# One list schedule for the whole attention part of a hybrid encoder block: every instruction recorded with a duration, ordered in the source, then issued

## The chip, the core and the metric

The kernel runs on one core of a Trainium2 chip. The core has five instruction queues that matter here: TensorE (PE, matrix products and transposes into PSUM), VectorE (DVE), ScalarE (ACT), GpSimd (POOL) and SyncE (SP, which here only issues transfers). Each queue runs its instructions in the order in which the program has them, and waits at an instruction until what it needs is there. The metric is the device time of one execution in microseconds (us); lower is better.

## The reference

One layer on x of 2048 rows by 1024 columns, float32:

```python
u = rms_norm(h, norm1_w)
proj = u @ w_in                     # 3072 columns: dq dk dv | sq sk sv
# differential attention, 4 heads: two softmax maps per head on QK-normed q, k,
# position bias by bucket, chunk-causal mask
p = softmax(logits); attn = p[0] - lam * p[1]; y_diff = rms_norm(attn @ dv) * (1 - lambda_init)
# stick-breaking attention, 8 heads, strictly causal, no softmax
log_1mb = where(mask, log_sigmoid(-z), 0)
rem = cumsum(log_1mb, reverse=True) - log_1mb
a = where(mask, exp(log_sigmoid(z) + rem), 0);  y_sb = rms_norm(a @ sv)
h = h + concat(y_diff, y_sb) @ w_out
h = h + (silu(rms_norm(h) @ w_gate) * (rms_norm(h) @ w_up)) @ w_down
```

## The kernel before

**Tiles.** Rows are cut into 16 tiles of 128 (`NT`). Every large product is made from float16 halves: an operand is split into a high half and a low half (what the high half leaves), and three products, high by high, high by low and low by high, are summed in PSUM. Splitting is therefore work of its own everywhere: a cast for the high half (ACT, at times DVE or POOL) and a subtract for the low half (DVE or POOL).

**Stages.** Attention runs over eight groups (`NG`). Groups 0 to 3 are one differential head each, groups 4 to 7 two stick-breaking heads each. For each group there are

- the group's 384 columns of W_in, loaded, scaled and split (tiles `wst`, `w16`);
- the projection: for each of 16 row tiles the halves of the normed x come back from a DRAM scratch (`xt<-xs`, on SP) and 24 matmuls make `pj` (PE); from it come `qT`, `kT`, `v` (transposed by DMA and split);
- scores: for each tile i of 128 queries and each piece of up to 1024 keys, matmuls `sc<-kT,qT` into PSUM (PE);
- the weights: in the differential groups bias, maximum, exponential with sums, reciprocal and the difference of the two maps (DVE line 695, ACT line 685); in the stick-breaking groups a sigmoid on ACT and a running product along the row on DVE (the scan of lines 1123 and following), right to left;
- the split of the weights into halves (`s<-z` or `s16`) and their transposition to `aT`, mostly by a DMA transpose on SP (`aT<-s`, `aT<-z`, line 590 and 1173), in groups 4 to 6 for narrow pieces by transposes on PE, a cast on ACT and a subtract on DVE (lines 1141, 1145, 1149);
- values: matmuls `yp<-v,aT` (PE line 646), some pieces later than the scores; then a norm per head, and the mix row to a DRAM scratch `ms`.

The projection of group g + 1 runs beside the attention of group g. Near the end of group 7's projection the output weights are loaded in four quarters (`load_wo`; `WT` names the projection tiles at which the first three begin); then the output projection `po<-wo,mt` (line 1433) adds x and stores h. The last four row tiles' output projection overlaps the feed-forward part, which splits its weights in steps (`wg`, `wu`, `wd`) and is bound to the projections `pm` and `pd`.

**What sets the order.** Three different things:

- groups 0 to 3, the start of group 4, all of group 7's attention, the output projection and the feed-forward part are written as plain code, and the framework's scheduler orders it, by program order, priorities (`PRI`) and its own estimate of times;
- from tile 8 of group 4's projection up to group 7's eighth projection tile, `planned(4, NG - 2)` lists the work as tasks, each with an engine, a duration in ns, what it depends on, rooms it takes and gives back (a room is a buffer of one name) and a key (its due time in units of a group). `Plan.order` simulates five engines and one DMA ring, always takes the task with the smallest key that is ready, and the tasks are issued in that order under a manual schedule. The engine of each task is fixed by hand there;
- in the plain code, where an operation may go to one of several engines (casts `to16`, subtracts `tt`), `pick` keeps a running load for each engine and takes the one that would be loaded least, with weights `KW`:

```python
def pick(**cost):
    e = min(cost, key=lambda k: load[k] + cost[k] * KW[k])
    load[e] += cost[e] * KW[e]
```

In group 7 a piece's weights are always turned by DMA: `split_t` casts on ACT, subtracts on POOL, and one DMA transpose on SP turns both halves, whatever the piece's width; the value matmuls of a piece stand behind the last score matmul in issue (`issue_after(front[-1])`).

Of the kernel before, what the change touches and what calls it, by code (L numbers as in the profile page):

```python
# [25 lines left out]
NFG = FF // 256  # L26
# [36 lines left out]
class Task:  # L63
    __slots__ = ("eng", "ns", "fn", "deps", "get", "put", "key", "dma", "left", "users", "at", "end")

    def __init__(self, eng, ns, fn, deps, get, put, key, dma):
        self.eng, self.ns, self.fn, self.deps, self.get, self.put, self.key, self.dma = eng, ns, fn, deps, get, put, key, dma


class Claim:  # L70
    def __init__(self, name, n=1):
        self.name, self.n = name, n


class Plan:


    def __init__(self, room):
        self.tasks, self.room = [], dict(room)

    def add(self, eng, ns, fn, deps=(), get=(), put=(), key=0.0, dma=None):
        t = Task(eng, ns, fn, [d for d in deps if d is not None], get, put, key, dma)
        self.tasks.append(t)
        return t

    def order(self):
        for n, t in enumerate(self.tasks):
            t.users, t.at = [], None
            t.left = len(t.deps)
            t.key = (t.key, n)  # L90
        for t in self.tasks:
            for d in t.deps:
                d.users.append(t)
        events = [(0.0, n, "ready", t) for n, t in enumerate(self.tasks) if not t.left]
        heapq.heapify(events)
        count = len(self.tasks)
        ready = {e: [] for e in "TADPS"}
        free = {e: True for e in ready}
        after = {t: 0.0 for t in self.tasks}
        ring, done = 0.0, []  # L100
        while events:
            now = events[0][0]
            while events and events[0][0] <= now:
                _, _, kind, t = heapq.heappop(events)
                if kind == "ready":
                    ready[t.eng].append(t)
                elif kind == "idle":
                    free[t] = True
                else:
                    for c in t.put:  # L110
                        c.n -= 1
                        if not c.n:
                            self.room[c.name] += 1
                    for u in t.users:
                        u.left -= 1
                        after[u] = max(after[u], now + (0 if u.eng == t.eng else LAT[t.eng]))
                        if not u.left:
                            count += 1
                            heapq.heappush(events, (after[u], count, "ready", u))
            for e in ready:  # L120
                if not free[e]:
                    continue
                for t in sorted(ready[e], key=lambda t: t.key):
                    need = {}
                    for n in t.get:
                        need[n] = need.get(n, 0) + 1
                    if all(self.room[n] >= k for n, k in need.items()):
                        break
                else:
                    continue  # L130
                for n, k in need.items():
                    self.room[n] -= k
                ready[e].remove(t)
                t.at = now
                done.append(t)
                free[e] = False
                end = now + t.ns
                if t.dma is not None:
                    ring = max(ring, now) + t.dma
                    end = max(ring, now + t.ns + DMA_LAG)  # L140
                t.end = end
                count += 2
                heapq.heappush(events, (now + t.ns, count - 1, "idle", e))
                heapq.heappush(events, (end, count, "end", t))
        assert len(done) == len(self.tasks), (len(done), len(self.tasks), self.room, [t.key for e in ready for t in ready[e]][:20])
        return done


def block(tc, a, out):
    nc = tc.nc  # L150
    PE, ACT, DVE, POOL, SP = nc.tensor, nc.scalar, nc.vector, nc.gpsimd, nc.sync
    top = ExitStack()
    with top:
        cp = top.enter_context(tc.tile_pool(name="cp", bufs=1))
        sm = top.enter_context(tc.tile_pool(name="sm", bufs=8))
# [18 lines left out]
        def to16(dst, src, n, engines="ADP", psum=False):  # L174
            cost = {"A": 0.84 * n + 110, "D": (1.05 if psum else 0.53) * n + 70, "P": 1.1 * n + 80}
            e = pick(**{k: cost[k] for k in engines})
# [7 lines left out]
        def tt(dst, a_, b_, op, n, engines="DP"):  # L184
            cost = {"D": 1.15 * n + 70, "P": 2.45 * n + 80}
            e = pick(**{k: cost[k] for k in engines})
            (DVE if e == "D" else POOL).tensor_tensor(dst, a_, b_, op)  # L187

        def pri(k):
            def deco(f):  # L190
                @functools.wraps(f)
                def g(*args):
                    with tc.high_priority(PRI[k]) if PRI[k] else nullcontext():
                        return f(*args)
# [12 lines left out]
        make_identity(nc, id32[:])  # L207
        mhalf = c1(16, "mh")
# [1745 lines left out]
```

## Time and profile before

| | before |
|---|---|
| median of 3 runs | 2679.03 us (2674.0 to 2679.57) |
| profiled execution | 2680.29 us |
| its span in the trace | 2678.5 us, 50436 instructions |
| granted PE clock, mean | 0.977 of full speed |
| busy: PE, DVE, ACT, POOL | 93%, 69%, 46%, 50% |

Times are of one profiled execution. The span is the time between the first and the last instruction in the trace; the execution's own time is 1.8 us longer. PE's busy share counts its matmuls and transposes; its weight loads (PEld) run beside them. A wait row names who waited, for what, and on which tile, with the total in us, the number of times and the longest. A window row gives, for a stretch of the span, each engine's busy time in it. "SPq" is SP as a queue of transfers, the only thing that it does.

### The profile page before, as it was taken

What the parts mean: (1) busy time and instruction counts of PE and PEld (TensorE: products, weight loads), DVE (VectorE), ACT (ScalarE), POOL (GpSimd) and SP (SyncE); (2) the same over time, 40 slices, a digit from 0 to 9 for tenths busy, and PEclk for the clock granted to TensorE, in tenths of its full rate; (3) what the DMA queues carried; (4) which work ended last, traced back from release to release, by engine and by line L of the source; (5) the groups of instructions that cost most, each with busy time, mean ns of one, the idle gap of its engine ahead of it and who ended that gap; (6) DMA issues with size and microseconds to landing.
All of it is one profiled execution on the core that took longest, in us unless ns stands there. A gap on an engine that the chain in (4) does not pass through costs nothing.

```text
span 2678.5 us, 50436 instructions
## 1 busy us (share of the span) xinstructions
PE 2489.6 (93%) x19876; PEld 1517.9 (57%) x19876; DVE 1851.8 (69%) x3400; ACT 1243.0 (46%) x2378; POOL 1340.4 (50%) x1024
## 2 busy tenths in 40 slices
PE   6998989887999989689989899999999999999999
PEld 4655656566787876468775344444444444444444
DVE  6888879896788888676656868777685444444434
ACT  4655656555677867464534535344352112111121
POOL 2568677763453545455554656565564232322323
PEclk8999999999999999899999899999999999999999
DMA  6777697766797979998897574665649744635532
GB/s 222 214 153 178 150 199 167 166 137 157 159 184 177 183 155 190 199 198 224 217 292 271 208 255 179 250 229 200 246 183 346 292 179 143 232 143 185 195 111 94
DMA packets 574653, 526.52 MB, mean 197 GB/s; under 512 B 431104, under 2 KB 503296, under 8 KB 564176
## 3 DMA queue, kind: packets, MB, share of 16 engines
q1 hardware_dynamic: 572592, 521.22, 69.0%
q8 instruction: 155, 2.54, 0.4%
q0 software_dynamic: 512, 1.36, 0.2%
q10 hardware_dynamic: 1312, 0.72, 0.1%
q14 instruction: 82, 0.67, 0.1%
HBM read 261.08 MB, written 147.32 MB: 152 GB/s over the span
## 4 chain that ended last, share of the span: by engine, by line
PE 40%; DVE 7%; issue 2%; DMA 1%; ACT 1%; POOL 1%; SPq 0%; DVEq 0%; ACTq 0%; POOLq 0%
PE pd L1746 15%; PE pm L1638 10%; PE pd L1638 7%; PE pa L1638 7%; PE po L1433 1%; DVE wd L298 1%; DVE wu L298 1%; DVE cg L1711 1%; PE fsc L1571 1%; DVE cg L187 0%; DVE wg L298 0%; DMA aT<-s 0%; DVE b L187 0%; DVE act L187 0%; ACT wu L293 0%
## 5 line engine op out<-in xcount | busy, mean ns | idle before, releaser
L1746 PE MATMUL pd<-wd,act 128*128 128x512 f16 x1764 | 390.5, 379 | 1.5 <-DVE cg L1679 1.4
L636 PE MATMUL sc<-kT,qT 128*128 128x512 f16 (+3 forms) x1280 | 326.3, 355 | 20.2 <-DVE z L671 5.1
L415 PE MATMUL pj<-w,xt 128*128 128x384 f16 x1728 | 324.3, 335 | 12.4 <-ACT xt L1284 5.2
L646 PE MATMUL yp<-v,aT 128*128 128x64 f16 (+1 forms) x4872 | 254.6, 205 | 64.6 <-DMA aT<-s 45.3
L1638 PEld LDWEIGHTS <-wg 128*128 128x128 f16 x1848 | 182.1, 99 | 225.6 <-issue 13.2
L1638 PEld LDWEIGHTS <-wu 128*128 128x128 f16 x1848 | 181.0, 98 | 220.0 <-issue 5.3
L646 PEld LDWEIGHTS <-aT 128*128 128x128 f16 x4896 | 228.6, 100 | 128.3 <-DMA aT<-s 59.6
L1746 PEld LDWEIGHTS <-act 128*128 128x128 f16 x1764 | 172.8, 98 | 209.2 <-issue 2.5
L187 POOL TENSOR_TENSOR s<-z,s 128x1024 f16<-128x1024 f32 (+7 forms) x144 | 241.4, 1686 | 84.2 <-ACT s L178 72.5
L187 POOL TENSOR_TENSOR act<-cg,act 128x512 f16<-128x512 f32 x112 | 148.5, 1336 | 263.6 <-ACT act L1705 151.5
L415 PEld LDWEIGHTS <-xt 128*128 128x128 f16 x1728 | 170.7, 100 | 132.0 <-issue 22.2
L187 POOL TENSOR_TENSOR hs<-hs,cu 128x512 f32<-128x512 f32 x99 | 130.9, 1330 | 170.3 <-DVE hs L1752 70.6
L1705 ACT CAST act<-cg 128x512 f16<-128x512 f32 x126 | 77.6, 618 | 239.4 <-DVE cg L1711 164.3
L1638 PE MATMUL pm<-X,wu 128*128 128x512 f16 x792 | 181.9, 382 | 3.3 <-DVE cg L1675 2.0
L1638 PE MATMUL pm<-X,wg 128*128 128x512 f16 x792 | 181.7, 382 | 0.0
L1164 POOL TENSOR_TENSOR z<-z,z 128x512 f16<-128x512 f32 (+3 forms) x96 | 102.4, 1069 | 152.8 <-ACT z L1160 140.5
L1752 DVE SCALAR_TENSOR_TENSOR hs<-pd,c,hs 128x512 f32<-128x512 f32 x136 | 98.8, 747 | 109.8 <-PE pd L1746 88.3
L671 DVE TENSOR_SCALAR_CACHE_REDUCE z<-sc,c 128x512 f32<-128x512 f32 (+3 forms) x256 | 161.1, 648 | 15.7 <-PE sc L636 14.9
L685 ACT ACTIVATE z<-z,ng 128x1024 f32<-128x1024 f32 (+4 forms) x192 | 170.7, 891 | 2.2
L1433 PEld LDWEIGHTS <-mt 128*128 128x128 f16 x1536 | 151.3, 100 | 34.4 <-issue 13.7
L636 PEld LDWEIGHTS <-qT 128*128 128x128 f16 x1280 | 110.9, 100 | 69.2 <-issue 19.7
L1433 PE MATMUL po<-wo,mt 128*128 128x256 f16 x1152 | 139.0, 277 | 7.4 <-DVE wo L1436 4.0
(344 smaller groups left out, 4994.0 us busy)
## 6 DMA issues: line engine op xcount, KB each, us to landing
xt<-xs SPq DMA_DIRECT2D x112, 512.0 KB, 4.4
hs<-hd SPq DMA_DIRECT2D x68, 512.0 KB, 4.6
hd<-hs SPq DMA_DIRECT2D x56, 512.0 KB, 4.8
split<-wg SPq DMA_DIRECT2D x11, 1792.0 KB, 7.8
split<-wu SPq DMA_DIRECT2D x11, 1792.0 KB, 6.7
split<-wd SPq DMA_DIRECT2D x11, 1792.0 KB, 6.9
wg<-split SPq DMA_DIRECT2D x11, 1792.0 KB, 7.2
wd<-split SPq DMA_DIRECT2D x11, 1792.0 KB, 11.5
```

What stands on the lines that cost most here:

```text
L187: (DVE if e == "D" else POOL).tensor_tensor(dst, a_, b_, op)
L415: last = PE.matmul(pj[:, :384], lhsT=xv[:, xi, kt, :], rhs=G["w"][:, wi, kt, :], start=n == 0, stop=n == 23)
L636: last = PE.matmul(sc[:, : 128 * w].rearrange("p (t n) -> p t n", n=P), lhsT=G["q"][i // 4][:, a_, i % 4, :], rhs=G["k"][q][:, b_, 0:w, :] ...
L646: PE.matmul(yp[:, y0 : y0 + wd], lhsT=aT[:, a_, :], rhs=v[:, v_ : v_ + wd], start=start and j == 0 and q == 0, stop=stop and j == nb - 1 a ...
L671: DVE.tensor_scalar(z[:, lo : lo + f], sc[:, :f], kz_d[:], None, op0=ALU.mult, op1=ALU.max, accum_out=mx[:, m, nx : nx + 1])
L685: ACT.activation(z[:, :n], z[:, :n], AF.Exp, bias=ng[:, m : m + 1], accum_out=(s2[:, m, b : b + 1] if nb > 1 else su[:, m : m + 1]))
L1164: POOL.tensor_tensor(u["s16"][:, nd + lo : nd + hi], src[:, so + lo : so + hi], u["s16"][:, lo:hi], ALU.subtract)
L1433: PE.matmul(po[:, sl], lhsT=mt[:, kt, P * xi : P * xi + P], rhs=wos[2 * h + n][wi][:, kt, :], start=q == 0, stop=q == 23)
L1638: front[0] = PE.matmul(ps_[:].rearrange("p (t n) -> p t n", n=P), lhsT=wv[:, wo, wi, 128 * kt : 128 * kt + 128], rhs=X[xo][:, :, xi, kt, : ...
L1705: ACT.copy(act[:, o, 0], src)
L1746: front[0] = PE.matmul(po[:], lhsT=act[:, ao, xi, 128 * j : 128 * j + 128], rhs=W["d"][:, wo, wi, :], start=start and u == 0 and q == 0, s ...
L1752: DVE.scalar_tensor_tensor(dst, po[:], kd[:], src, op0=ALU.mult, op1=ALU.add)
```

## The change

All of the attention part, from the start of the kernel to the output projection, is now first taken down and then issued. `Recorder` stands between the code and the engines: while it is on, each engine call makes an `Op` with a duration from `price`, a table by engine, operation, width, source (PSUM or SBUF) and table function; its dependencies are found by who last wrote and who still reads each element of each tile (`Bank`, `View`). PE's matmuls into one PSUM tile are tied into pieces of up to 680 ns. `order` is one simulation of five engines for the whole list, and `issue` calls the real engines in its order under a manual schedule:

```diff
+PIECE, LOOK = 680.0, 60
-PRI = {"sc": 0, "spl": 0, "pv": 0, "fin": 0, "pm": -200, "po": 0, "pb": 0, "lw": 0, "fr": 0, "at": 200, "ox": 0, "wm": 0}
+PRI = {"sc": 400, "spl": 400, "pv": 0, "fin": 0, "pm": -200, "po": 400, "pb": 400, "lw": 0, "fr": 400, "at": 200, "ox": 0, "wm": 0}
-WT = (8, 9, 10)
+WT = (4, 7, 10)
-KW = {"A": 1.0, "D": 1.0, "P": 1.0}
+KW = {"A": 1.0, "D": 2.5, "P": 0.6}
...
+    def price(self, eng, name, args, kw):
...
+            if name == "dma_start_transpose":
+                return 1000 + 0.375 * width(src), 222.0 * width(src) / P, None, False
...
+            if name == "tensor_tensor_scan":
+                return 110 + 2.29 * n, None, None, False
...
+            return 180 + 1.07 * n, None, None, not psum and name != "tensor_reduce"
...
+            for e in ready:
+                if till[e] > now:
+                    continue
...
+                for o in ready[e][:LOOK]:
+                    if not can(o):
+                        continue
...
+                    if o.alts:
+                        w = way(o, e, now)
...
+                    if w[4] if w else o.port:
+                        if shared > now:
+                            if e == "D" and want is None:
+                                want = o.key
+                            continue
...
+                if o.table is not None and o.table != table:
+                    table = o.table
+                    ns += 1300
+                end = till[e] = now + ns
...
+                if o.dma is not None:
+                    ring = max(ring, now) + o.dma
+                    end = max(ring, now + ns + DMA_LAG)
```

An engine that is free takes, among the first 60 ready operations by key (program order less the priority's boost), the first whose tiles have a free buffer (`can`). The model knows one DMA ring with 2300 ns from issue to landing, 1300 ns for a change of ACT's function table, and a port: an operation of DVE on SBUF alone and one of POOL on SBUF are not run at the same time (`port`, `shared`). Where an operation may go to several engines (`either`), the engine is chosen when it is ready, by who would end first, with the durations weighted by `KW` (`way`): an operation's time counts 2.5 times on DVE and 0.6 times on POOL.

`planned`, `Plan` and `Task` are gone; groups 4 to 7 all come from the plain code of `sb_attn`. There narrow pieces are turned on PE in all four groups, and `issue_after` is gone:

```diff
+            def turn_on(m, n):
+                return n <= 512 or (n < 1024 and m == 1)
...
-                        front.append(score_chunk(G, sc, i, 2 * b + c, m, w // P))
+                        score_chunk(G, sc, i, 2 * b + c, m, w // P)
...
-                    return n, split_t(om[:, :n], n, "A", "P", wide[0] if g < NG - 1 else None, g)
...
+                        if tee and c == 0:
+                            for k in range(nb):
+                                PE.transpose(sc[:, P * k : P * k + P], om[:, P * k : P * k + P], id32[:])
...
+                            ACT.copy(h_, sc[:, :w])
+                            DVE.tensor_tensor(l_, sc[:, :w], h_, ALU.subtract)
+                            continue
...
-                    with tc.issue_after(front[-1]):
-                        stage_c(i, m, b, n, aT)
...
-                        planned(4, NG - 2)
...
+            rec.issue()
```

In group 7 these are 64 transposes on PE, 22 casts on ACT and 22 subtracts on DVE, for 16 DMA transposes less. ACT has five table loads for three before. The feed-forward part is still ordered by the framework, and its `pick` uses the new `KW`; 14 of its subtracts `act<-cg,act` go from DVE to POOL.

Three places show what moves. In the rows a name is a tile and its number, then what is read, then partitions and elements; the new instructions of the attention part all have the line of `issue`, 514.

DVE, where the differential groups hand over to the stick-breaking groups. `z<-z,rc,z` is the difference of two softmax maps, `z<-sc,diag` the first scan of group 4, `qT`, `yk` and `v` are low halves of projections. Before:

```order
L695 SCALAR_TENSOR_TENSOR z_8151<-z_8170,rc_8198,z_8151 128x1024
L695 SCALAR_TENSOR_TENSOR z_8160<-z_8179,rc_8198,z_8160 128x1024
L484 SCALAR_TENSOR_TENSOR qT_7980<-pj_8257,qT_7980 64x256
L484 SCALAR_TENSOR_TENSOR v_7979<-sd_8331,v_7979 128x4x64
L484 SCALAR_TENSOR_TENSOR yk_8139<-pj_8257,kT_7981 64x256
L484 SCALAR_TENSOR_TENSOR vr_7324<-pj_8258,vr_7324 128x4x64
L484 SCALAR_TENSOR_TENSOR qT_7980<-pj_8257,qT_7980 64x256
L484 SCALAR_TENSOR_TENSOR yk_8139<-pj_8257,kT_7981 64x256
L898 SCALAR_TENSOR_TENSOR v_7979<-sd_8546,v_7979 128x4x64
L1123 SCALAR_TENSOR_TENSOR z_8555<-sc_8556,diag 128x128
```

And now:

```order
L514 SCALAR_TENSOR_TENSOR z_7989<-z_8179,rc_8410,z_7989 128x1024
L514 SCALAR_TENSOR_TENSOR z_8075<-z_8220,rc_8410,z_8075 128x896
L514 TENSOR_SCALAR z_8483,mx_8283<-sc_8351,c_189 128x512
L514 TENSOR_SCALAR z_8483,mx_8283<-sc_8384,c_189 128x256
L514 ISA z_8483,mx_8283<-sc_8384,bias,c_189 128x256
L514 ISA mx_8283 128x1
L514 TENSOR_REDUCE ng_8536<-mx_8283 128x2
L514 SCALAR_TENSOR_TENSOR yrs_8539<-yss_7479,er_7616 128x4
L514 SCALAR_TENSOR_TENSOR qT_8534<-pj_8314,qT_8534 64x256
L514 SCALAR_TENSOR_TENSOR z_8558<-sc_8412,diag 128x128
```

Before, the first scan stands behind the last difference of maps and a row of projection halves; now it stands in the middle of the last differential pieces, and two more differences of maps follow 26 rows behind it.

SP, in group 7 where the output weights come in (`z<-in_w_out_dram`). `xt<-xs` are the operands of the next projection tiles. Before:

```order
L1173 DMA_TRANSPOSE aT_17525<-z_17434 128x16x128
L1173 DMA_TRANSPOSE aT_17529<-s_17496 128x16x128
L590 DMA_TRANSPOSE aT_17663<-s_17660 128x2x128
L590 DMA_TRANSPOSE aT_17678<-s_17675 128x2x128
L590 DMA_TRANSPOSE aT_17689<-s_17686 128x4x128
L590 DMA_TRANSPOSE aT_17700<-s_17697 128x4x128
L1048 DMA qT_17450<-qT_17450 64x1024 x2
L1404 DMA z_17746<-in_w_out_dram 128x4x256
L1404 DMA z_17747<-in_w_out_dram 128x4x256
L1404 DMA z_17844<-in_w_out_dram 128x4x256
L1404 DMA z_17845<-in_w_out_dram 128x4x256
L237 DMA bias<-in_norm_w_dram 128x1024
```

And now:

```order
L514 DMA xt_17615<-xs 128x2048
L514 DMA_TRANSPOSE aT_17623<-s_17532 128x16x128
L514 DMA z_17727<-in_w_out_dram 128x4x256
L514 DMA z_17731<-in_w_out_dram 128x4x256
L514 DMA xt_17798<-xs 128x2048
L514 DMA xt_18001<-xs 128x2048
L514 DMA_TRANSPOSE aT_18017<-s_17848 128x10x128
L514 DMA_TRANSPOSE aT_18023<-s_17876 128x2x128
L514 DMA_TRANSPOSE qT_18040<-st_17493 128x8x128
L514 DMA_TRANSPOSE kT_18059<-st_17493 128x8x128
L514 DMA bias<-in_norm_w_dram 128x1024
L514 DMA ms<-mo_18047 128x2x256
```

The narrow transposes (2 and 4 blocks) at the head of group 7 are gone from the queue, and the quarters of the output weights stand apart, with projection operands between them.

POOL, at the end of the attention part. `x<-z,x` are low halves of the feed-forward part's operands, `sx`, `sq` and `wg<-stages` the first gate weight. Before:

```order
L187 TENSOR_TENSOR x_20989<-z_20976,x_20989 128x2x512
L233 TENSOR_TENSOR xrs_21248<-xrs_21248,mh_68 128x1
L187 TENSOR_TENSOR x_21390<-z_21244,x_21390 128x2x512
L187 TENSOR_TENSOR sx_21467<-stages 128x512
L233 TENSOR_TENSOR xrs_21373<-xrs_21373,mh_68 128x1
L187 TENSOR_TENSOR z_21389<-z_21245 128x512
```

And now:

```order
L514 TENSOR_TENSOR z_21259<-z_21476,z_21259 128x512
L220 TENSOR_SCALAR wg_21534<-stages,c_21531 128x2x512
L220 TENSOR_SCALAR wg_21534<-sx_21551,c_21531 128x512
L514 TENSOR_TENSOR x_21480<-z_21455,x_21480 128x2x512
L514 TENSOR_TENSOR x_21482<-z_21476,x_21482 128x2x512
L220 TENSOR_TENSOR sq_21532<-stages,sq_21532 128x512
```

POOL now has two wide subtracts of operands next to each other there, and the first gate weight's work stands between the operands' rows.

More of the change, by code (lines that the diff above doesn't have):

```diff
@@ L129, in order @@
                 else:
                     continue
[L131 to L141, printed above, removed]
+                for b in o.first:
+                    queue[b.slot].remove(b)
+                    room[b.slot] -= 1
@@ L207, in block @@
         make_identity(nc, id32[:])
+        rec.start()
         mhalf = c1(16, "mh")
```

890 lines of the change are left out of this document (415 added, 475 removed).

## The prediction

> **What bounds the kernel now.** I read the page's head and its busy shares first, then the table of busy time by stage, then TensorE's (PE's) own waits in each stage, and last the rows of the operations that the change moves.
>
> ```profile
> span 2678.5 us, 50436 instructions
> PE 2489.6 (93%) x19876; PEld 1517.9 (57%) x19876; DVE 1851.8 (69%) x3400; ACT 1243.0 (46%) x2378; POOL 1340.4 (50%) x1024
> ```
>
> PE is the busiest engine by far, but 93% is a mean over two unlike halves, so the table by stage decides. Its columns are the stage's length, then busy time (and instructions) of PE, PE's weight loads, DVE, ACT and POOL, then the granted clock, the DMA share and GB/s. I cut where the kind of work changes: start, four differential groups, the change to the stick-breaking groups, groups 4 to 6, group 7 as the output weights come in, the output projection, the first feed-forward step, and the rest.
>
> ```profile
> 0.00:67.00 67.00, 45.31 (x233) 28.14 (x234) 43.78 (x117) 31.08 (x60) 17.90 (x32) 0.90 0.70 222
> 67.00:603.00 536.00, 485.83 (x4074) 321.27 (x4072) 463.41 (x1331) 318.22 (x828) 375.15 (x269) 0.98 0.76 171
> 603.00:670.00 67.00, 51.39 (x747) 46.29 (x745) 44.33 (x96) 35.68 (x83) 25.20 (x19) 0.92 0.64 159
> 670.00:1072.00 402.00, 369.69 (x5876) 308.08 (x5875) 342.24 (x479) 291.65 (x603) 195.04 (x181) 0.98 0.88 175
> 1072.00:1206.00 134.00, 104.43 (x1092) 72.15 (x1090) 89.42 (x144) 72.17 (x146) 63.62 (x50) 0.87 0.92 197
> 1206.00:1430.00 224.00, 206.25 (x2113) 175.69 (x2111) 135.50 (x191) 101.27 (x149) 114.56 (x77) 0.98 0.86 251
> 1430.00:1541.00 111.00, 100.08 (x478) 48.74 (x476) 82.98 (x118) 59.25 (x77) 67.63 (x44) 0.94 0.63 225
> 1541.00:2678.50 1137.50, 1126.57 (x5279) 517.52 (x5277) 650.09 (x932) 333.67 (x437) 481.30 (x357) 1.00 0.55 204
> ```
>
> From 1541 us on PE is 99% busy at full clock: the feed-forward part is bound by PE and gives nothing. What a better order can win lies ahead of 1430 us. I call a stage's loss PE's idle time plus PE's busy time times the missing clock: start 21.7 + 4.5 = 26.2; differential groups 50.2 + 9.7 = 59.9; the change of kind 15.6 + 4.1 = 19.7; groups 4 to 6, 32.3 + 7.4 = 39.7; group 7, 29.6 + 13.6 = 43.2; output projection 17.8 + 4.1 = 21.9. Together 210.6 us. Per microsecond, group 7 (32%) and the change of kind (29%) are worst, the two stretches at whose edges the old program hands over from one scheduler to the other. PE's own waits, stage by stage (start; 67 to 603; 603 to 670; 670 to 1072; 1072 to 1206):
>
> ```profile
> PE wsc L260 <- DVE xrs L232: 11.7, 1, 11.7
> ...
> PE yp L646 <- DMA aT<-s: 28.7, 24, 4.2
> ...
> PE wsc L830 <- DVE yk L898: 6.0, 1, 6.0
> PE sd L909 <- ACT vr L481: 3.0, 1, 3.0
> PE pj L870 <- DMA xt<-xs: 1.6, 1, 1.6
> ...
> PE yp L646 <- DMA aT<-z: 16.9, 13, 2.5
> PE yp L646 <- DMA aT<-s: 4.5, 5, 1.9
> ...
> PE osc L260 <- ACT wo L267: 7.1, 2, 4.8
> PE yp L646 <- DMA aT<-s: 6.8, 3, 3.3
> PE sc L636 <- DVE v L484: 4.3, 1, 4.3
> PE yp L646 <- DMA aT<-z: 2.0, 2, 1.6
> ```
>
> (us in total, times, longest.) In the long stages PE waits for one thing above all: the value matmuls `yp` stand in its queue ahead of the landing of their transposed weights `aT`.
>
> **The change, part by part.**
>
> *Start: 0.* The 11.7 us are the loads of x and of the first weight and the norm behind them; the new order has the same rows there. Ends -4 to +4.
>
> *Differential groups: -14.* No operation is added but the choice of engine. Between a piece's last score matmul and its first value matmul stand 219 matmuls in the median before and 220 now, and 130 against 116 in the closest tenth. So the 28.7 us of waiting do not go by distance. What can go is part of the other 21.5 us of idle time and of the clock's 9.7, by DVE and POOL work taken in better turn. I take a half of those, 15.6, less a little for the closer tenth. Ends: -40 (half of the 59.9 and ten more) and +15 (half as much waiting again).
>
> *Change of kind: -8.* The 6.0 and 3.0 us go, since the new DVE order has group 4's first scans ahead of the last differential pieces. Against it ACT changes its table twice more (five loads in its order, three before):
>
> ```profile
> L1108 ACT ACT_TABLE_LOAD x1 | 1.3, 1283 | 0.0
> ```
>
> That is 2.6 us on an engine 53% busy there; 1 of it I let through. Ends -15 and +3.
>
> *Groups 4 to 6: -24.* Same operations, but 280 matmuls in the median between scores and values for 190 before, and 187 at the least for 84. A matmul row of this stage starts every 56 ns or faster, so 90 more are up to 5 us, twice the longest wait of 2.5. I take the 21.4 us as gone, with 3 of the 7.4 for the clock. The next to be late are DVE, 85% busy, and the DMA engines, 88%: room for 402 x 0.12 = 48 us, enough. Ends -35, and +10 if those two take all of it back.
>
> *Group 7: -18.* It now turns the narrow pieces on PE, as groups 4 to 6 do. Added are 64 transposes, 22 casts on ACT and 22 subtracts on DVE that read PSUM; removed are 16 DMA transposes and the halves' casts and subtracts on ACT and POOL. The rows:
>
> ```profile
> 828.40 0.60 PE L1141 MATMUL sc<-id,z 128*128 128x128 f32 x4
> 828.84 0.83 PE L870 MATMUL pj<-xt,w 128*128 128x128 f16 x12
> ...
> L1149 DVE TENSOR_TENSOR aT<-sc,aT 128x512 f16<-128x512 f32 x30 | 20.4, 679 | 13.0 <-ACT aT L1145 12.9
> ...
> 1096.21 8.13 SPq L590 DMA_TRANSPOSE aT<-s  x4
> ```
>
> Four transposes hold PE from 828.40 to 828.84, 0.11 us each: 64 cost 7.0 us of PE. The DVE subtracts are at most 22 x 0.68 = 15 us on an engine 67% busy there, beside PE. Each narrow DMA transpose holds the SP queue 2.0 us, so 16 give 32 us back in a stage where SP issues one after the other and DMA is at 0.92. With the output weights' loads spread and begun earlier (tiles 4, 7, 10 for 8, 9, 10), and 347 matmuls for 213 ahead of the values, the waits of 7.1, 6.8, 4.3 and 2.0 go, 20.2, and 5 of the clock's 13.6: -25, and with the 7 added -18. Ends -35 and +5.
>
> *Output projection: -4*, a fifth of its 21.9. Ends -12 and +10.
>
> *First feed-forward step: +6.* The weights of the choice (DVE 2.5, POOL 0.6) hold there too, and in the output projection the new rows give POOL the operand subtracts that DVE shared:
>
> ```profile
> L187 POOL TENSOR_TENSOR x<-z,x 128x1024 f16<-128x1024 f32 x10 | 22.9, 2287 | 13.9 <-ACT x L178 13.9
> ...
> L187 DVE TENSOR_TENSOR x<-z,x 128x1024 f16<-128x1024 f32 x8 | 13.4, 1685 | 1.6 <-POOL x L182 1.6
> ...
> 1414.07 5.40 PE po L1433 x48
> ```
>
> Eight of 2.29 us move to POOL. POOL's rows for the last pair of tiles, with the first gate weight between them, come to some 23 us in one queue; the cover is the last four projection tiles, each 96 matmuls or 10.8 us of PE, 43 us. It holds for the operands, but the first up and down weights follow in the same queue later than now, and 1430 to 1541 already loses 10.9 us. Without the cover it would be all of 23; I take 6. Ends -5 and +20.
>
> Sum: 0 - 14 - 8 - 24 - 18 - 4 + 6 = -62. Against the profiled execution's own 2680.29 us (span 2678.5 and 1.8 around it) that is 2618. The median shown is 2679.03, 1.3 lower, so 2617.
>
> **A rule that speaks against it.** DVE and POOL stretch each other in the differential groups (min/median/max ns):
>
> ```profile
> L695 DVE SCALAR_TENSOR_TENSOR z<-z,rc,z x96: 337/1270/3061, 111.8 to 617.2; 128x1024 f32<-128x1024 f32 x40, 128x128 f32<-128x128 f32 x8, 128x256 f32<-128x256 f32 x8, 128x384 f32<-128x384 f32 x8
> ...
> L695 DVE SCALAR_TENSOR_TENSOR z<-z,rc,z 128x1024 f32<-128x1024 f32 x40 | 65.1, 1636 | 0.6
> ...
> L187 POOL TENSOR_TENSOR s<-z,s x92: 425/1892/3645, 113.1 to 602.7; 128x1024 f16<-128x1024 f32 x37, 128x128 f16<-128x128 f32 x8, 128x256 f16<-128x256 f32 x8, 128x384 f16<-128x384 f32 x8
> ```
>
> The widest of L695 have a mean of 1.64 us where the median of all sizes is 1.27, and go up to 3.06. The Trainium skill, page "SBUF — State Buffer", section "Who interferes with whom", says that a DVE instruction with two SBUF inputs and a GpSimd instruction that reads SBUF shut each other out, the later one blocking whole. The trace agrees: 3.06 is one such operation and a POOL subtract's 1.89 in a row, nearly. By that rule the choice that prefers POOL costs DVE time; what it would make of the total is the second rival.
>
> **The rivals.**
>
> 1. *Slower: the SP queue.* All loads and transposes stand in one order on SP, and each waits there for its maker:
>
> ```profile
> SPq L590 <- POOL s L187: 141.4, 54, 11.5
> ```
>
> If a POOL subtract comes later than planned, the x-tile load behind its transpose comes late, and PE's projection stops. The stretch is up to 3.65 - 1.89 = 1.75 us a time; there are 112 loads of x tiles. It decides when more than 62 / 1.75 = 35 of them are late; with 60 late it adds 105 us: 2617 + 105 = 2722. For it: those 141 us of waiting. Against it: PE lost only 1.6 us to such a load at 603 to 670. Chance 0.13.
>
> 2. *Port.* If each of the 96 L695 waits half a POOL subtract, 0.95 us, it is 91 us in place of the 15 of now (40 x 0.37), and DVE would have 463 + 76 = 539 us in a stage of 536. At DVE's 0.86 of now some of it is taken from its idle time, and the stage would be about 36 us longer than now in place of 14 shorter: 2617 + 50 = 2667. Chance 0.12.
>
> 3. *No change.* PE's waits turn into waits for DVE: 463 + 44 + 342 us of work from 67 to 1072 at the same 0.85, so nothing from there, and group 7's and the change's -26 eaten by 15 us of added subtracts and 6 at the end: 2674. The change does what it says, but DVE was the bound. Chance 0.07.
>
> 4. *Much faster.* All loss but the start's goes down to the 1% of the feed-forward part: 210.6 - 26.2 - 12 = 172 less, 13 added: 2521. Chance 0.13, since 28.7 us of waits at unchanged distance speak against it.
>
> **How the numbers follow.** The forecast, 2617 with its own range of 2565 to 2665 (the terms' ends, not all on one side), has the other 0.55. The range given reaches from 2550, above the whole of rival 4, to 2682, which holds rivals 2 and 3 and leaves out rival 1: about 0.2 outside. A measurement here tells about 0.2%, 5 us, from no change. Faster: the forecast, rival 4, rival 2 but for its upper tail (0.10), and a quarter of rival 3: 0.80. Within it: 0.06. Slower: rival 1 and a bit of 3: 0.14.
>
> **What would show it.** Right: from 670 us on no `yp` wait for `aT` of over 10 us in total; the stretch of group 7 with a clock of 0.95 or more; first feed-forward product near 1360 us for 1425 now; idle in the differential groups still led by `yp` behind `aT`. Rival 1 would show as PE `pj` waits for `xt`; rival 2 as L695's means above 2 us; rival 3 as DVE over 95% busy. Wrong altogether: a wait of a kind that no row above has, such as a buffer that the new order frees late.

## The result: 25 us faster, where 62 were forecast

The changed kernel takes 2653.03 us (median of 6 runs, 2651.68 to 2662.01), the kernel before 2677.93 in the same sittings (6 runs). The ratio is 0.9923, with a 95% interval of 0.9902 to 0.9943. The forecast was 2617.

The head of the changed kernel's page and its busy shares:

```profile
span 2650.7 us, 50621 instructions
PE 2475.5 (93%) x19940; PEld 1510.4 (57%) x19940; DVE 1834.4 (69%) x3398; ACT 1224.7 (46%) x2365; POOL 1412.5 (53%) x1093
```

POOL has 72 us more to do than before (1340.4), the others a little less. PE's share is the same 93%, so the head says nothing about where the time went. For that I cut both traces where PE has done the same work: each matmul counted at its steady time (29 ns for 64 columns, 56 for 128, up to 216 for 512), and behind the middle of group 7 the 7 us of the added transposes allowed for. The stages between these cuts, to the last matmul:

| stage | before, us | changed, us | difference | forecast |
|---|---|---|---|---|
| start | 79.6 | 78.0 | -1.6 | 0 |
| differential groups | 522.7 | 525.0 | +2.3 | -14 |
| change of kind | 73.3 | 55.6 | -17.7 | -8 |
| groups 4 to 6 | 396.0 | 389.0 | -7.0 | -24 |
| group 7, output weights | 146.1 | 130.7 | -15.4 | -18 |
| output projection | 216.8 | 207.3 | -9.5 | -4 |
| first feed-forward step | 67.9 | 76.9 | +9.0 | +6 |
| the other steps | 1171.5 | 1183.6 | +12.1 | 0 |

Two kernels whose attention part is issued in the same order (the changed one and the first experiment) differ by 4.5 us in the differential groups, so differences below 5 us in a stage aren't read. In the output projection, kernels that differ in the feed-forward part's weights alone lie further apart: the changed one and the first experiment by 9.3 us, the kernel before and the second experiment by 5.4, shorter with the new weights both times. Weights for weights the change makes that stage 0.3 and 4 us shorter, so its 9.5 aren't read as a gain of the new order. The table by stage of the changed kernel at these cuts (length, then busy time of PE, its weight loads, DVE, ACT, POOL, the granted clock, DMA share, GB/s):

```profile
78.00:603.00 525.00, 472.39 (x4010) 314.00 (x4008) 440.90 (x1315) 316.42 (x798) 337.65 (x246) 0.98 0.80 172
603.00:658.60 55.60, 51.26 (x798) 46.13 (x796) 46.43 (x111) 36.00 (x80) 25.66 (x19) 1.00 0.63 138
658.60:1047.60 389.00, 362.17 (x5763) 300.07 (x5760) 331.74 (x475) 285.19 (x594) 187.90 (x172) 1.00 0.91 184
1047.60:1178.30 130.70, 115.65 (x1331) 85.34 (x1328) 108.13 (x182) 87.47 (x184) 59.74 (x54) 0.97 0.93 201
```

At the change of kind PE is 92% busy at full clock (77% at 0.92 before), and group 7's clock went from 0.87 to 0.97. The differential groups stand where they stood, with DVE 84% busy. PE's waits there, from 78 to 603 us (total, times, longest):

```profile
PE yp L514 <- DMA aT<-s: 13.4, 12, 2.8
PE sc L514 <- DVE z L514: 6.5, 8, 2.0
PE sc L514 <- DVE mx L514: 5.3, 6, 1.9
PE yp L514 <- DVE y L514: 5.3, 4, 3.4
PE yp L514 <- DVE mo L514: 4.7, 3, 3.5
```

The wait for transposed weights is half of what it was (28.7), and waits for DVE stand in its place: all of them together are 36.2 us, for 9.9 between the cuts of the kernel before. Groups 4 to 6, 658.6 to 1047.6:

```profile
PE sc L514 <- DVE z L514: 9.6, 12, 2.0
PE yp L514 <- DMA aT<-z: 4.3, 3, 1.7
PE pj L514 <- DVE qT L514: 2.7, 5, 0.9
PE sc L514 <- DVE aT L514: 2.2, 4, 0.8
PE yp L514 <- DMA aT<-s: 2.1, 2, 1.9
```

21.4 us of waiting for `aT` became 6.4, and about half of it came back as waits for DVE (10.5 us before, 18.3 now). In the feed-forward part, from 1385.6 on, PE's waits are 35.0 us, for 17.2 from 1434.5 on before. One row of before, then the longest now:

```profile
PE fsc L1571 <- ACT sq L1562: 5.9, 1, 5.9
```

```profile
PE fsc L220 <- ACT sq L220: 10.3, 3, 9.2
PE pd L220 <- DVE xrs L220: 7.0, 1, 7.0
PE pd L220 <- DMA X<-xcd: 5.1, 1, 5.1
PE pd L220 <- ACT cg L220: 4.3, 2, 3.6
PE pd L220 <- DVE hs L220: 3.7, 2, 2.3
```

### The profile page after: what moved, and what is told of

Its sections match the earlier page's. It is cut to its first block, busy times and chain, and to the rows that moved or that the text cites. A ratio compares the mean times of both kernels' runs of the same rounds, so it can differ in the third digit from the quotient of the medians.

```text
span 2650.7 us, 50621 instructions
## 1 busy us (share of the span) xinstructions
PE 2475.5 (93%) x19940; PEld 1510.4 (57%) x19940; DVE 1834.4 (69%) x3398; ACT 1224.7 (46%) x2365; POOL 1412.5 (53%) x1093
## 4 chain that ended last, share of the span: by engine, by line
PE 53%; DVE 11%; POOL 8%; DMA 7%; issue 6%; ACT 5%; SPq 0%; DVEq 0%; POOLq 0%; ACTq 0%
PE pd L220 18%; PE pj L514 9%; PE pm L220 8%; PE pa L220 5%; PE sc L514 5%; PE yp L514 4%; DMA aT<-s 3%; DVE z L514 3%; PE po L514 3%; POOL s L514 2%; DVE cg L220 2%; DVE wd L220 2%; ACT z L514 1%; DVE wu L220 1%; POOL sq L220 1%
## 5 line engine op out<-in xcount | busy, mean ns | idle before, releaser
L514 PE MATMUL pj<-w,xt 128*128 128x384 f16 (+1 forms) x3072 | 435.6, 288 | 10.5 <-DVE w L514 6.4
L514 POOL TENSOR_TENSOR s<-z,s 128x512 f16<-128x512 f32 (+7 forms) x231 | 301.2, 1316 | 134.2 <-ACT s L514 113.0
L514 PE MATMUL sc<-kT,qT 128*128 128x512 f16 (+3 forms) x1280 | 320.7, 350 | 31.7 <-DVE z L514 22.4
L514 PEld LDWEIGHTS <-xt 128*128 128x128 f16 x3072 | 255.9, 99 | 142.7 <-issue 18.5
L220 POOL TENSOR_TENSOR act<-cg,act 128x512 f16<-128x512 f32 x126 | 172.8, 1382 | 272.9 <-ACT act L220 160.8
L514 PE MATMUL yp<-v,aT 128*128 128x64 f16 (+1 forms) x4872 | 235.9, 204 | 28.6 <-DMA aT<-s 17.4
L514 PEld LDWEIGHTS <-aT 128*128 128x128 f16 x4896 | 218.6, 99 | 63.3 <-DMA aT<-s 25.8
L220 POOL TENSOR_TENSOR hs<-hs,cu 128x512 f32<-128x512 f32 x99 | 130.7, 1328 | 171.3 <-DVE hs L220 71.6
L514 POOL TENSOR_TENSOR z<-z,z 128x512 f16<-128x512 f32 (+4 forms) x108 | 117.5, 1090 | 150.3 <-ACT z L514 135.0
L514 DVE TENSOR_TENSOR_SCAN z<-z,sc 128x512 f32<-128x512 f32 x128 | 162.2, 1273 | 14.2 <-ACT z L514 10.7
L514 PE MATMUL pj<-xt,w 128*128 128x128 f16 x2304 | 152.8, 219 | 13.1 <-DVE qT L514 4.4
```

Source lines behind the costliest of these rows:

```text
L220: return f(*map(true, args), **{k: true(v) for k, v in kw.items()})
L514: o.out = f(*map(true, args), **{k: true(v) for k, v in kw.items()})
```

## Experiments

Three questions: what took the gain of the differential groups and of groups 4 to 6, what the feed-forward part lost, and which part of the change made what was gained. The ratios are to the kernel before, with 95% intervals.

**1. The feed-forward part's weights.** The choice of engine goes back to the old weights behind the attention part:

```diff
             rec.issue()
+            KW.update(A=1.0, D=1.0, P=1.0)
```

> The changed kernel lost 21 us in the feed-forward part against before (28 us ahead at the end, 49 ahead at the first down product). Here the weights of the choice of engine go back to 1, 1, 1 after the attention part is issued, so the feed-forward part chooses as before. Theory W (the weights do it): 12 to 21 us of it come back, 2632 to 2641 us, and PE's waits in the feed-forward part fall below 20 us. Theory H (the hand-over from the issued list to the framework's order does it): within 4 us of the changed kernel, 2649 to 2657.

2646.04 us, ratio 0.9896 (0.9880 to 0.9913), 7 us less than the changed kernel. That lies between the two theories, and the intervals of the two ratios overlap, so the total decides nothing. The stages do: the steps behind the first come back whole (+0.5 us against before, +12.1 in the changed kernel), and the first loses 3.0 us for 9.0. In this profile the output projection was 9 us longer than the changed kernel's, 7 of it in one wait (this run, then the changed kernel):

```profile
PE po L220 <- DVE wo L220: 10.1, 3, 8.2
```

```profile
PE po L220 <- DVE wo L220: 3.1, 2, 2.2
```

These are the last row tiles, which overlap the feed-forward part, so the old weights may have cost that; experiment 2 has the same sign, and no run shows the way. Theory W for the steps behind the first.

**2. The same weights in the kernel before:** new weights at the start of its feed-forward part, nothing else.

> The kernel before, with the new weights of the choice (DVE 2.5, POOL 0.6) in the feed-forward part alone. Theory W: slower than before by 10 to 20 us, 2688 to 2698. Theory H: within 4 us of before, 2674 to 2682.

2694.33 us, ratio 1.0080 (1.0065 to 1.0096). The steps behind the first get 17.2 us longer. Theory W, from the other side: DVE counted 2.5 times sends work to POOL (1422.1 us busy, 1340.4 before), in a part that PE had filled to 99%.

**3. Durations without the overlap.** The schedule's table charges an instruction with its length in a profile. The timeline of the changed kernel's DVE shows what that is (start, length):

```profile
302.14 0.75 DVE L514 TENSOR_SCALAR_CACHE_REDUCE z<-sc,c 128x512 f32<-128x512 f32 x1
302.81 0.09 DVE L514 DVE_READ_ACCUMULATOR z<-sc,c 128x1 f32 x1
302.81 0.75 DVE L514 TENSOR_SCALAR_CACHE_REDUCE z<-sc,c 128x512 f32<-128x512 f32 x1
303.48 0.08 DVE L514 DVE_READ_ACCUMULATOR z<-sc,c 128x1 f32 x1
```

The second scaled maximum starts 0.67 us after the first, which lasts 0.75 and is followed by a read of 0.09: instructions that stand back to back overlap by some 80 ns on DVE. The table has 828 ns for this one. In the list's own simulation (what it believes, no measurement) DVE was therefore 99% full from 60 to 1010 us; in the trace it was 84% busy. The Trainium skill, page "Perfetto Trace Analysis", section "Optimizing Scalar/DVE Operations", says that a profiled latency holds about twice the engine's busy overhead, because the half that acknowledges the write overlaps with the next instruction. The trace agrees that neighbours overlap, by a median of 82 ns on DVE and 98 on ACT; the factor of two isn't seen in these rows. The edit takes it out of the table and puts it into the way to the next user:

```diff
-LAT = {"T": 250.0, "A": 120.0, "D": 120.0, "P": 120.0, "S": 100.0}
+LAT = {"T": 250.0, "A": 250.0, "D": 240.0, "P": 120.0, "S": 100.0}
+SAME = {"T": 0.0, "A": 130.0, "D": 120.0, "P": 0.0, "S": 0.0}
...
-            t = 195 + 0.84 * n + (40 if f is not None else 0) + (190 if kw.get("accum_out") is not None else 0)
+            t = 55 + 0.84 * n + (40 if f is not None else 0) + (190 if kw.get("accum_out") is not None else 0)
...
-                return 110 + 2.29 * n, None, None, False
+                return 15 + 2.29 * n, None, None, False
...
-                return (290 if kw.get("accum_out") is not None else 150) + (1.05 if psum else 0.55) * n, None, None, not psum
+                return (135 if kw.get("accum_out") is not None else 40) + (1.05 if psum else 0.55) * n, None, None, not psum
...
-            return 180 + 1.07 * n, None, None, not psum and name != "tensor_reduce"
+            return 60 + 1.07 * n, None, None, not psum and name != "tensor_reduce"
```

> The changed kernel with shorter durations for DVE and ACT in the schedule's table: back to back, the trace shows the next instruction begin some 80 ns (DVE) and 100 ns (ACT) ahead of the end of the one before, and the table charges some 120 and 140 ns per instruction more than that. The difference moves into the latency to the next user. By the table of the changed kernel DVE is 99% full in the schedule from 60 to 1010 us; with these it is 85%. Theory B (the list was bound by a DVE that is only full on paper): faster by 15 to 50 us, 2603 to 2638, by the differential groups and groups 4 to 6. Theory A (DVE is full in truth): within 6 us of the changed kernel, 2647 to 2659.

2603.28 us, ratio 0.9740 (0.9720 to 0.9760): 50 us faster than the changed kernel. Theory B. The differential groups are 44.4 us shorter than before (changed: 2.3 longer), group 7 28.5 (15.4); groups 4 to 6 get 3.6 (7.0), no more, though I had expected a gain there too. The differential groups here, by stage and by PE's waits:

```profile
79.20:557.50 478.30, 462.13 (x3988) 306.98 (x3986) 433.54 (x1333) 318.84 (x809) 333.96 (x231) 1.00 0.85 184
```

```profile
PE sc L515 <- DVE mx L515: 5.8, 7, 2.5
PE sc L515 <- DVE z L515: 5.6, 6, 2.5
PE yp L515 <- DMA aT<-s: 3.1, 5, 1.3
```

PE is 97% busy at full clock and the waits for `aT` are nearly gone. DVE does the same work in 47 us less time, and is 91% busy. The edit shortens ACT's durations along with DVE's and lengthens the ways between engines. That the longer ways made the gain is ruled out by experiment 7, which shortens them again and loses nothing; DVE's durations alone, without ACT's, no run has tried.

**4. Is DVE full in truth?** Each combine of the two maps works on half its columns, with the order kept:

```diff
-DVE.scalar_tensor_tensor(z0[:, :n], z1[:, :n], rc[:], z0[:, :n], op0=ALU.mult, op1=ALU.add)
+half = DVE.scalar_tensor_tensor(z0[:, : n // 2], z1[:, : n // 2], rc[:], z0[:, : n // 2], op0=ALU.mult, op1=ALU.add)
+half.ns = 180 + 1.07 * n
```

> The changed kernel, but each of the differences of the two softmax maps on DVE works on the left half of its columns alone (the right half stays as it is), at the same duration in the schedule, so that the order stays. About 40 to 50 us of DVE work leave the differential groups. Theory A (DVE is full there in truth): the differential groups get shorter by 25 us or more, 2613 to 2630 in all. Theory B (DVE has slack there, the list is what binds): by less than 10 us, 2643 to 2655.

2650.61 us, ratio 0.9918 (0.9900 to 0.9936), 2 us less than the changed kernel. The same stretch of PE's work:

```profile
78.00:595.40 517.40, 469.99 (x4011) 312.94 (x4009) 407.59 (x1316) 315.13 (x798) 328.24 (x247) 0.98 0.80 174
```

DVE is 33 us less busy there and the stage 8 us shorter: theory B again. In the order as issued DVE waits for others where the list, with DVE 99% full, thought it working. Its longest wait in the changed kernel, from 67 to 603:

```profile
DVE v L514 <- ACT raw L514: 29.5, 27, 2.8
```

**5. Groups 4 to 6.** On the kernel of experiment 3, each running product that continues a row does half its columns, with the order the same row for row:

```diff
-DVE.tensor_tensor_scan(ov, ov, sc[:, :w], carry, op0=ALU.mult, op1=ALU.bypass)
+half = DVE.tensor_tensor_scan(ov[:, w // 2 :], ov[:, w // 2 :], sc[:, w // 2 : w], carry, op0=ALU.mult, op1=ALU.bypass)
+half.ns = 15 + 2.29 * w
```

> The kernel with the prices without overlap (2603 us), but each running product that continues a row on DVE works on the left half of its columns alone, at the same duration in the schedule, so that the order is the same row for row. Groups 4 to 6 (393 us there, DVE busy 336) lose 144 halves of 0.59 us, some 84 us of DVE work; group 7 another 28. Theory D (DVE sets the pace of groups 4 to 6): that stage gets shorter by 15 us or more, 2570 to 2590 in all. Theory L (what is left there is PE's matmuls and the many short ways between engines): by 6 us or less, 2595 to 2608.

2598.72 us, ratio 0.9711 (0.9682 to 0.9739), 5 us less than experiment 3. The stage without and with the edit:

```profile
613.40:1005.80 392.40, 363.37 (x5888) 302.87 (x5886) 335.08 (x473) 290.10 (x598) 196.05 (x175) 1.00 0.91 185
```

```profile
617.20:1003.30 386.10, 360.97 (x5889) 302.38 (x5887) 270.82 (x474) 287.99 (x598) 195.42 (x175) 1.00 0.94 188
```

64 us of DVE's work less shorten it by 6: theory L, at the edge of its bound. DVE's amount of work doesn't set the pace there, though PE's waits are on DVE. PE's 25 us of idle time that stay are many short waits; which way between engines they hang on is open.

**6. Both causes taken away:** experiment 3 and the line of experiment 1.

> The prices without overlap and, behind the attention part, the weights of the choice back at 1, 1, 1. If the two causes add: 7 to 10 us below 2603, 2593 to 2597, with the feed-forward part's own loss at 10 to 14 us for 23 now. If the loss there belongs to the hand-over alone: 2600 to 2606.

2591.34 us, ratio 0.9684 (0.9663 to 0.9705), 12 us below experiment 3. They add, by a little more than the 7 to 10 that I expected. The steps behind the first are as long as before (-0.1 us, +13.4 in experiment 3); the first one still loses 4.6. PE's waits from 1337 us on:

```profile
PE pd L221 <- DVE cg L221: 10.2, 4, 5.5
PE fsc L221 <- ACT sq L221: 5.9, 1, 5.9
PE pd L221 <- DMA X<-xcd: 3.5, 2, 2.5
```

The 7.0 for `xrs` is gone, and `fsc` waits once for 5.9 us as it did before.

**7. The ways between engines as measured, too:**

```diff
-LAT = {"T": 250.0, "A": 250.0, "D": 240.0, "P": 120.0, "S": 100.0}
+LAT = {"T": 250.0, "A": 150.0, "D": 140.0, "P": 80.0, "S": 100.0}
```

> The kernel at 2591 us (prices without overlap, old weights in the feed-forward part), with the way from one engine to the next in the schedule also at what the trace shows: 32 to 77 ns behind an end of ACT, 55 behind one of DVE, 34 to 77 behind one of POOL, so 150, 140 and 80 ns behind the end of the priced part for 250, 240 and 120. Theory M (each truer number helps): 3 to 12 us faster, 2579 to 2588. Rival N (what is left are PE's own matmuls and chance): within 3 us, 2588 to 2594.

2581.42 us (2580.36 to 2584.29), ratio 0.9651 (0.9637 to 0.9666): the fastest version, 72 us faster than the changed kernel. Against experiment 6 it is 10 us by the medians, while the intervals of the ratios just meet, so theory M holds with its size uncertain.

**8 to 10. The port.** `order` keeps DVE's work on SBUF and POOL's apart. Without that, first on experiment 3, then on the changed kernel itself:

```diff
-                    if w[4] if w else o.port:
+                    if False:
```

> The prices without overlap, but the schedule lets DVE and POOL work on SBUF at the same time (the port is not modelled). Theory P (keeping the two apart is worth something): the combines of 128x1024 on DVE go from a mean of 1.44 us to 1.6 or more, as before, and the time up by 5 to 15 us, 2608 to 2618. Rival (the freedom gained makes up for it): 2597 to 2607.

2663.53 us, ratio 0.9952 (0.9936 to 0.9969): 60 us slower than experiment 3, though the combines didn't get longer (1.34 us for 1.44). Theory P in the time, with four times the price that I expected, and not by the sign that I named: DVE was given 15 low halves `s<-z,s` for 4, and 10 `st<-raw,st` for 1.

> The changed kernel as it was, but its schedule lets DVE and POOL work on SBUF at the same time. With the prices without overlap this cost 60 us, by some 30 low halves that went to DVE and were stretched there. If the port is what counts: 25 to 60 us slower than the changed kernel, 2678 to 2713, slower than before too. If it counts only once DVE looks free (here DVE is 99% full in the schedule, so little is given to it): within 12 us, 2645 to 2665.

2705.05 us, ratio 1.0103 (1.0080 to 1.0127): 52 us slower than the changed kernel and slower than before. The low halves on DVE and the widest combines, by line and shape, here and then in the changed kernel:

```profile
L514 DVE TENSOR_TENSOR s<-z,s 128x384 f16<-128x384 f32 (+4 forms) x16 | 30.2, 1884 | 1.8 <-POOL s L514 1.6
L514 DVE SCALAR_TENSOR_TENSOR z<-z,rc,z 128x1024 f32<-128x1024 f32 x40 | 58.7, 1475 | 1.1
```

```profile
L514 DVE TENSOR_TENSOR s<-z,s 128x256 f16<-128x256 f32 x1 | 0.4, 424 | 1.3 <-ACT s L514 1.3
L514 DVE SCALAR_TENSOR_TENSOR z<-z,rc,z 128x1024 f32<-128x1024 f32 x40 | 53.6, 1347 | 0.7
```

A low half, of 128 to 640 columns in these rows, takes 1.88 us on DVE in the mean; the only one in the changed kernel, of 256 columns, took 0.42. One by one in the trace, 13 of the 16 take 1.3 to 2.7 us. Each of these began while a low half of 1024 columns was already running on POOL, and ended 0.15 to 0.68 us behind it. The other three take 0.41 to 0.56; one of them lies beside nothing on POOL, two beside POOL's small `rs<-rs,mh` (128x16). To part the choice from the order, the third run forbids DVE for them:

```diff
-                return rec.either([ways[e] for e in engines])
+                return ways["P"]()
```

> The changed kernel without the port in its schedule (2705 us), and the low halves that may go to DVE or POOL all go to POOL, as nearly all do in the changed kernel. So the choice is that of the changed kernel, and only the order lets DVE and POOL meet. Theory C (the 52 us are the choice: some 20 low halves on DVE, stretched to 1.9 us each): within 12 us of the changed kernel, 2641 to 2665. Theory O (they are the meetings themselves): 25 us or more slower than the changed kernel, 2678 or more, with the combines of 128x1024 on DVE at 1.5 us or more for 1.35.

2689.27 us, ratio 1.0060 (1.0041 to 1.0078): 36 of the 52 us stay. Theory O by the time; its sign, 1.5 us or more for the widest combines, did not come. They, and casts that the edit leaves free, which the changed kernel doesn't have on DVE:

```profile
L514 DVE SCALAR_TENSOR_TENSOR z<-z,rc,z 128x1024 f32<-128x1024 f32 x40 | 57.3, 1440 | 1.1
L514 DVE CAST st<-raw 128x512 f16<-128x512 f32 x4 | 5.4, 1342 | 0.3 <-POOL raw L514 0.3
L514 DVE CAST x<-z 128x512 f16<-128x512 f32 (+1 forms) x2 | 4.0, 2002 | 0.4 <-POOL z L514 0.4
L514 DVE CAST s<-z 128x128 f16<-128x128 f32 (+2 forms) x4 | 2.9, 718 | 0.0
```

40 combines that are 93 ns longer are 4 us, not 36. Ten casts for high halves have come to DVE, 12 us of work, so the choice isn't quite the changed kernel's either. Some 16 us are the choice of low halves; of the other 36 the runs show that the port in the schedule is worth them, not through which operations. For the low halves the Trainium skill's page "SBUF — State Buffer", section "Who interferes with whom", has the rule (whichever of the two comes later is blocked whole), and the 13 above agree: each waited out a POOL instruction that had begun before it. The two beside `rs<-rs,mh` weren't held up.

**11. Group 7 turned by DMA, as before:**

```diff
-                return n <= 512 or (n < 1024 and m == 1)
+                return g < NG - 1 and (n <= 512 or (n < 1024 and m == 1))
```

> The changed kernel, but in group 7 all pieces are turned by DMA, as before; the rest of the change stays. Theory T (turning the narrow pieces on PE is what group 7 gains by): 10 to 20 us slower than the changed kernel, 2663 to 2673. Rival S (one list over the border of group 7 and the spread loads are what it gains by): within 6 us of it, 2647 to 2659, with 64 fewer transposes paying for what the DMA costs.

2669.70 us, ratio 0.9978 (0.9965 to 0.9991), 17 us slower than the changed kernel: theory T. Group 7's stage is 2.1 us shorter than before, for 15.4 in the change. In this profile, 6 us above the median, some 10 us more were lost in the feed-forward steps behind the first, which the edit doesn't touch.

**12. The old tiles for the output weights:** `WT = (8, 9, 10)`.

> The changed kernel, but the output weights are loaded at projection tiles 8, 9 and 10 of group 7 again. The spread counts (the prediction's reason): 5 to 12 us slower than the changed kernel, 2658 to 2665, in the stretch of group 7. It doesn't: within 4 us, 2649 to 2657.

2668.76 us, ratio 0.9979 (0.9969 to 0.9989), 16 us slower than the changed kernel: the spread counts, by more than I expected. Group 7 is then 2.2 us longer than before. So neither half of the change to group 7 gives anything alone. Each of these two edits also gives the whole list another order, and no run parts that from the edit itself. PE's largest wait there, with the DMA transposes, with the old tiles, and in the changed kernel:

```profile
PE sc L514 <- DVE z L514: 17.4, 20, 2.4
```

```profile
PE sc L514 <- DVE z L514: 12.3, 13, 3.4
```

```profile
PE sc L514 <- DVE z L514: 8.4, 10, 1.8
```

## Why the prediction was wrong

Its direction and several signs were right; three terms of the sum were not. Together they fell short by 45 us (16, 17 and 12). The change of kind, a term half the size that was measured, and the output projection, whose difference goes with the feed-forward weights and not with the order, gave 15 of them back; that the total is nearer than its terms is luck.

- **Differential groups, -14 forecast, +2 measured.** The step that failed is "DVE and POOL work taken in better turn". I took half of the other idle time for removable by any list, and didn't ask what the list itself believes to be full. Its table had DVE at 99%, by lengths that count the overlap of neighbours twice, which left it little freedom to take work in better turn. Experiment 3 shows it, as far as DVE's and ACT's durations can be taken together: with truer ones the same list gains 44 us there. Experiment 4 shows that DVE's work itself isn't the bound. The other half of the term was wrong too: "the 28.7 us of waiting do not go by distance" left them standing; the change kept the distance and they fell to 13.4 all the same, and to 3.1 in experiment 3, so distance alone didn't make them.
- **Groups 4 to 6, -24 forecast, -7 measured.** The waits for `aT` went as forecast: 21.4 us became 6.4, and the sign I named (under 10 us from 670 on) came: 6.4 here and 0.9 in the output projection. That the distance of 280 matmuls did it isn't shown, since in the differential groups they halved without it. That "the next to be late are DVE" with room enough was the fault: room in DVE's sum of work is no promptness. Waits of at most 2.0 us for a single scan or projection half took the place. Experiments 3 and 5 show that neither truer durations nor 64 us less of DVE's work end them; what would is open.
- **The feed-forward part, +6 forecast, +21 measured.** The first step was about right (+9), though thirteen operand subtracts moved to POOL there and not eight. The others I put at 0, "bound by PE and gives nothing". That it gives nothing doesn't mean that it can lose nothing: the changed weights hold in its every step. I had counted what moves to POOL and priced it at the hand-over alone. Experiments 1, 2 and 6 give 12 to 17 us for it.
- **Right:** the start; group 7 (-15 for -18; clock 0.97, as named), by transposes on PE and the spread loads, though as a pair (experiments 11 and 12), while I had the two as separate gains. Of the four waits that were to go there, 0.3 us is left. **Right in kind, wrong in size:** the change of kind, whose two waits went as told, with twice the gain (-18 for -8), since the clock came back there too (0.92 to 1.00), which I hadn't counted; no run takes that stage apart. The output projection (-9.5 for -4) isn't borne out: with the old weights in the feed-forward part and the same attention order it was 0.3 us shorter than before (experiment 1). The first feed-forward product came at 1378 us for the forecast 1360.
- **The rivals.** SP's queue didn't decide: no wait of `pj` for `xt` is among PE's leading ones. The port (rival 2) didn't happen in the change, since the list keeps the two engines apart: the combines got shorter (1.64 to 1.35 us) where I had them longer. The list's port isn't the whole reason, for without it they still took 1.48 and 1.44 us (experiments 9 and 10). That the list models it I had read and given no price; experiment 9 shows that without it the kernel would have been slower than before. Rival 3, with DVE as the bound, described the differential groups and groups 4 to 6 in time (-4.7 us together, the change of kind between them apart), but not in cause: its sign, DVE over 95% busy, didn't come (84% and 85%); DVE was full on paper only. "Idle in the differential groups still led by `yp` behind `aT`" came by the longest single row (13.4), while the waits for DVE together are 36.2.
- **Two readings in the working** were off without moving the sum: the start, not group 7, loses most per microsecond (26.2 of 67); and matmuls of groups 4 to 6 start every 68 ns in the mean (402 us for 5876), so 90 more of them are some 6 us, not up to 5.

## What to carry to other kernels

A list schedule can be no better than the engine that its table wrongly holds for full: before believing or judging one, compare each engine's share in the plan with the share in a trace, and price an instruction by the distance from its start to the next one's start, the rest as latency. A weight that steers a choice in one part of a kernel must not leak into a part that it wasn't tuned for; a part that is 99% bound by one engine has little to win, and here lost 12 to 17 us. A wait that goes is only worth what the next one behind it leaves, and free time in a neighbour's sum says little about whether it comes in time.

## What the runs showed of the hardware

Back to back, DVE's instructions overlap by some 82 ns and ACT's by 98 (medians); for a 128x512 scaled maximum with its read that is 0.67 us from start to start for a table's 0.83. A low half on DVE, two inputs from SBUF and 128 to 640 columns, took 1.88 us in the mean in a schedule without the port (16 of them), where the 1024-column combine of the schedule with it took 1.35. The 13 long ones all began behind a 1024-column subtract on POOL and ended 0.15 to 0.68 us after it; two beside POOL's work on 128x16 took 0.41 and 0.56.
